# Two blocks' mixer projections as half products in the last input pass

## The chip, the cores and the metric

The kernel runs on one core of one Trainium2 chip. The metric is the device time of one execution in microseconds; lower is better. Times named "runs" are medians of several executions. The profile comes from one execution of its own.

## The reference

One layer of an encoder over 2048 tokens of width 1024. Attention and an mLSTM work side by side on a shared input projection; each has its own output projection and its own gate; their sum goes through w_out, and an FFN follows.

```python
xn = rms_norm(x, mix_norm_g)
proj = xn @ w_in
aq, ak, av, mq, mk, mv, mo, ipre, fpre, ga, gm = jnp.split(proj, points, axis=-1)
att = chunk_band_attention(aq, ak, av, rel_bias)            # (2048, 512)
mlstm_out = sigmoid(mo) * rms_norm(mlstm_chunkwise(...))    # (2048, 512)
y = sigmoid(ga) * (att @ w_att_proj) + sigmoid(gm) * (mlstm_out @ w_mlstm_proj)
x = x + y @ w_out
x = x + square(relu(rms_norm(x) @ w_up)) @ w_down
return rms_norm(x, final_norm_g)
```

All is float32. The change is about the two products `att @ w_att_proj` and `mlstm_out @ w_mlstm_proj`, each of 512 by 1024 weights, for the first 1024 tokens.

## The kernel before

**Tiling.** The tokens are four blocks of 512 (0 to 3); blocks 0 and 1 are stage s = 0, blocks 2 and 3 are s = 1. Activations lie feature by token in tiles of 128 x 512. A float32 factor is kept as two parts, a rounded one (ScalarE's cast) and the rest (a subtraction on VectorE), and each product is three matmuls: high by high, high by low, low by high. An `r` tile holds both parts of one operand row, a `wsp` tile both parts of 1024 weight columns. Splitting costs a ScalarE and a VectorE operation, for weights (L501, L503) as for activations (L1109 with L1114, or with a factor of a half L1111 with L1116).

**Seven products.** Most big products are made for two blocks at once by seven products of half-size operands instead of eight: the weights and the activations are each cut into 2 x 2, sums and differences of the parts are formed, seven products are accumulated in three kinds of banks (x, y and z of PLACES), and the four results a11, a12, a22 and a21 come out of `combine` with three ScalarE copies and three VectorE adds for each row tile. Sums of weights are made on the chip ahead of time by `sum_w` (from the table SUMS: pass and item at which the work is started, priority 3) and put into DRAM (`wsum`). Sums of activations are made by `take_parts`: for one k it takes five tiles, makes four loads one after the other, forms four sums, and hands seven parts to a splitter.

**The order of work.** A planner (class Flow) runs at build time. Every piece of work is a generator that asks for an engine with an assumed duration, for buffers from a pool, or for an event; the planner gives engines to the request that can start first, with a priority, and the instructions are written in that order; some reordering afterwards is left to the layer beneath. A load asks for the SP queue for 0.8 us (256 KB) and counts as landed 2 us later, so loads that follow one another in one generator are planned 2.8 us apart. TensorE's main work is one generator, `dense`, with the lowest priority; attention and the mLSTM recurrence (`mixers`) fill in between.

**The stages.** `dense` begins with v for blocks 0 and 1, then nine quads of the first input stage (IN_FIRST), then `in_far`, the second input stage: ten items (IN_ORDER: gm0, gm1, q, mq, vm, ga0, k, mk, ga1, mo) in three passes (g = 0, 1, 2), with products 0, 3 and 1, then 2 and 4, then 5 and 6. Half results between the passes are parked in DRAM and brought back by `unpark`, one after the other, with at most `room` tiles ahead. The activations of a pass sit in `ring`, 16 of the 28 r tiles. During the passes, the mixers of blocks 0 and 1 run, and their results are stored row by row in DRAM (`keep_mix`, L1298).

**The projections.** PROJ_IN puts the projection of block 0 before item 6 of pass 1 and that of block 1 before item 5 of pass 2. `project` (L562 to L564 through `pair_tile`) takes eight split rows (`take_mix`, `load_mix`, `take_u1`), goes over eight weight tiles of 24 matmuls, and `merge` (L992, L1000) multiplies with the gates, adds the branches and stores y. After block 1's, `take_y` (L1715, L1765, L1111, L1116) is started for four k to make the operands of w_out's quads (L631), which follow `in_far`. For k = 2 and 3 it brings the parts 0 and 1 first (`ahead`).

**Pools.** There are 28 r tiles (`rpool`), 16 `ctx` tiles, six `temp`, four `sc`, three `wsp`, four `wraw` (weights as loaded), and eight PSUM banks.

## Time and profile before

| what | value |
|---|---|
| time, median of 3 runs | 2738.43 us (2737.99 to 2741.09) |
| time of the profiled execution | 2734.73 us |
| its span in the profile | 2732.9 us |
| PE busy | 2717.4 us, 12832 matmuls |
| DVE (VectorE) busy | 2074.9 us |
| ACT (ScalarE) busy | 1527.6 us |
| DMA | 672.53 MB, mean 246 GB/s |

How to read it: PE is TensorE's matmul, PEld its weight load, SP the engine that issues nearly all DMAs. Busy time is the time in which an engine has an instruction in work. A row of a group reads: line, engine, operation, output <- inputs, tile sizes, count | busy us, mean ns of one | idle us before them and what ended most of it. A row of the waits reads: who waited at which line <- for whom: us in all, times, longest. A row of the timeline gives start, duration, engine, line, operation and tiles. A row of the stretches gives, after the bounds and length in us, the busy us and instruction counts of PE, PEld, DVE, ACT and POOL, TensorE's granted clock (1.00 is full), the share of time the DMA engines are busy, and GB/s.

### The profile page before, as it was taken

The numbers are of one execution on the slowest core, as the hardware profiler recorded it, in microseconds if no ns is written. First come the engines' busy times: TensorE is split into PE (matmuls) and PEld (weight loads), VectorE is DVE, ScalarE is ACT, GpSimd is POOL, SyncE is SP. The second block draws the span as 40 slices with busy tenths as digits, with TensorE's granted clock in tenths as the row PEclk, the third lists the DMA queues.
The fourth block names the chain that finished last, engine by engine and source line by source line (L and its number), as shares of the span: only waits on it lengthen the run. The fifth ranks groups of instructions, "written<-read, shape, count | busy, mean of one in ns | idle before, by whom it ended". The sixth has DMA issues, their size and how long they took to land.

```text
span 2732.9 us, 38055 instructions
## 1 busy us (share of the span) xinstructions
PE 2717.4 (99%) x12832; PEld 2262.6 (83%) x12832; DVE 2074.9 (76%) x3685; ACT 1527.6 (56%) x2650; POOL 48.2 (2%) x79
## 2 busy tenths in 40 slices
PE   9999999999999999999999999999999999999998
PEld 8878888888888888888888888888888888888887
DVE  7868776788875778897767798879888665657675
ACT  6545446676742534566556776666445565554443
POOL 0000000000000000000000000000000000000000
PEclk9999999999999999999999999999999999999999
DMA  8877678888868889767768876877774454588863
GB/s 297 280 257 259 243 266 280 269 250 266 281 215 271 306 307 303 239 216 261 254 230 279 277 254 204 255 229 245 252 233 160 154 204 158 185 276 272 286 234 138
DMA packets 331240, 672.53 MB, mean 246 GB/s; under 512 B 36788, under 2 KB 66100, under 8 KB 331044
## 3 DMA queue, kind: packets, MB, share of 16 engines
q1 hardware_dynamic: 330324, 669.03, 73.0%
q8 instruction: 101, 1.65, 0.2%
q10 hardware_dynamic: 720, 1.06, 0.1%
q14 instruction: 95, 0.78, 0.1%
HBM read 458.27 MB, written 211.68 MB: 245 GB/s over the span
## 4 chain that ended last, share of the span: by engine, by line
PE 90%; DVE 6%; issue 1%; DMA 1%; ACT 1%; POOL 0%; SPq 0%; POOLq 0%; DVEq 0%; ACTq 0%
PE bank L631 37%; PE bank L662 11%; PE bank L562 9%; PE bank L563 9%; PE bank L564 9%; PE bank L667 3%; PE bank L1337 2%; PE bank L1262 2%; PE bank L1369 2%; PE bank L856 1%; DVE wsp L503 1%; DVE r L1114 1%; DMA x<-ctx 1%; PE bank L1420 1%; PE bank L1597 1%
## 5 line engine op out<-in xcount | busy, mean ns | idle before, releaser
L631 PE MATMUL bank<-r,wsp 128*128 128x512 f32 x4872 | 1110.6, 390 | 1.9 <-ACT r L1109 1.1
L631 PEld LDWEIGHTS bank<-r,wsp 128*128 128x128 f32 x4872 | 912.6, 188 | 194.9 <-ACT r L1109 1.8
L501 ACT CAST wsp<-wraw 128x1024 fp32r<-128x1024 f32 x439 | 461.3, 1051 | 540.9 <-PE bank L563 203.7
L503 DVE TENSOR_TENSOR wsp<-wraw,wsp 128x1024 fp32r<-128x1024 f32 x439 | 536.1, 1221 | 277.8 <-ACT wsp L501 271.8
L562 PE MATMUL bank<-r,wsp 128*128 128x512 f32 x1088 | 430.4, 396 | 0.0
L563 PE MATMUL bank<-r,wsp 128*128 128x512 f32 x1088 | 425.0, 391 | 1.6 <-DVE r L1287 1.6
L564 PE MATMUL bank<-r,wsp 128*128 128x512 f32 x1088 | 424.7, 390 | 0.0
L662 PE MATMUL bank<-r,wsp 128*128 128x512 f32 x1512 | 368.5, 393 | 1.3 <-DVE ctx L755 0.8
L662 PEld LDWEIGHTS bank<-r,wsp 128*128 128x128 f32 x1512 | 278.9, 188 | 58.3 <-DVE ctx L755 1.5
L564 PEld LDWEIGHTS bank<-r,wsp 128*128 128x128 f32 x1088 | 204.2, 188 | 43.6
L563 PEld LDWEIGHTS bank<-r,wsp 128*128 128x128 f32 x1088 | 204.6, 188 | 40.4 <-DVE r L1287 2.0
L562 PEld LDWEIGHTS bank<-r,wsp 128*128 128x128 f32 x1088 | 204.3, 188 | 38.5 <-DVE r L1374 0.3
L1114 DVE TENSOR_TENSOR r<-r 128x512 fp32r<-128x512 f32 x271 | 179.8, 688 | 16.1 <-ACT r L1109 13.4
L1109 ACT CAST r<-r 128x512 fp32r<-128x512 f32 x271 | 157.9, 617 | 31.0 <-DMA r<-u 27.6
L1798 DVE TENSOR_TENSOR ctx<-bank,ctx 128x512 f32<-128x512 f32 x150 | 103.0, 687 | 64.1 <-PE bank L631 64.0
L520 DVE TENSOR_TENSOR wraw<-wraw,wraw 128x1024 f32<-128x1024 f32 x112 | 136.2, 1219 | 3.8 <-DMA wsum<-wraw 2.8
L1350 ACT ACTIVATE sc<-sc,scs 128x640 f32<-128x640 f32 (+4 forms) x128 | 97.5, 762 | 67.1 <-DVE scs L1343 66.4
L2119 ACT ACTIVATE ctx<-ctx 128x512 f32<-128x512 f32 x96 | 60.5, 630 | 105.7 <-DVE ctx L1798 105.6
L1790 ACT COPY ctx<-bank 128x512 f32<-128x512 f32 x150 | 87.3, 582 | 53.4 <-PE bank L631 51.3
L1374 DVE TENSOR_TENSOR r<-bank,r 128x512 fp32r<-128x512 f32 (+1 forms) x168 | 95.6, 593 | 14.5 <-ACT r L1372 13.8
L1372 ACT CAST r<-bank 128x512 fp32r<-128x512 f32 (+1 forms) x168 | 80.9, 515 | 31.3 <-PE bank L1369 29.3
L1262 PE MATMUL bank<-r,r 128*128 128x512 f32 x336 | 95.2, 365 | 0.0
(257 smaller groups left out, 3060.6 us busy)
## 6 DMA issues: line engine op xcount, KB each, us to landing
wraw<-in_wf SPq DMA_DIRECT2D x196, 512.0 KB, 4.4
r<-u SPq DMA_DIRECT2D x224, 256.0 KB, 4.2
wraw<-wsum SPq DMA_DIRECT2D x104, 512.0 KB, 4.5
u<-ctx SPq DMA_DIRECT2D x128, 256.0 KB, 2.4
u<-tmp SPq DMA_DIRECT2D x96, 256.0 KB, 2.4
wraw<-in_w SPq DMA_DIRECT2D x47, 512.0 KB, 4.4
ctx<-in_wf SPq DMA_DIRECT2D x88, 256.0 KB, 3.9
wsum<-ctx SPq DMA_DIRECT2D x88, 256.0 KB, 3.4
```

The source lines that it names most:

```text
L501: nc.scalar.copy(w[:, 0], raw)
L503: nc.vector.tensor_sub(w[:, 1], raw, w[:, 0].bitcast(F32))
L520: V.tensor_sub(dst, x, y)
L562: mm(ps, lh, rh, start=first, stop=False)
L563: mm(ps, lh, rl, start=False, stop=False)
L564: mm(ps, ll, rh, start=False, stop=last)
L631: mm(ps, wv[:, x, k, n], a[:, y], start=new and k == 0 and x == y == 0, stop=k == 3 and x == 1, skip_group_check=True)
L662: mm(ps, wv[:, x, k, n], a[:, y], start=start and x == y == 0, stop=stop and x == 1, skip_group_check=True)
L1109: self.nc.scalar.copy(dst[:, 0], src)
L1114: self.nc.vector.tensor_sub(dst[:, 1], src, dst[:, 0].bitcast(F32))
L1262: nc.tensor.matmul(bkv[:, :, c0:c0 + w], st, sl[:, :, o:o + w], start=n == 0, stop=n == total - 1)
L1798: nc.vector.tensor_add(t[:, o:o + 512], ps, t[:, o:o + 512])
```

## The change

The projections of blocks 0 and 1 are no longer made block by block. For each branch (x = 0 attention, x = 1 mLSTM) both blocks' rows are taken together as 2 x 2 parts, and seven products give the four results; as the contraction is only 512 long, a product has two k tiles instead of four, and two products share one weight tile. A branch is done in two halves q of the output columns. Branch 0 comes before item 1 (gm1) and branch 1 before item 4 (vm) of pass 2 (JOINT). The operands of both branches are made by `take_joint`, one branch and one k after the other, from the rows in DRAM, beginning with pass 2. The gated results of branch 0 are kept in four sc tiles and in six r tiles (through SP) until branch 1's are added. The sums of the two new weight matrices are made in the first input stage (SUMS at items 4 and 6). `take_y` becomes `take_y_late` for these blocks: each k waits until all seven parts of the k before it are there. The loads for pass 2's own products are started at the beginning of pass 1, and `unpark` may be eight tiles ahead in both passes, twelve after the second joint product.

```diff
@@ -46,7 +46,7 @@
 N_G, N_O, N_F = 2, 2, 8
 N_Q = N_G + N_O + 2 * N_F
 
-Q_VM = N_Q
+Q_VM, Q_PJ = N_Q, N_Q + 9
 Q_IN = dict(q=N_Q + 2, mq=N_Q + 3, ga0=N_Q + 4, k=N_Q + 5, mk=N_Q + 6, ga1=N_Q + 7, mo=N_Q + 8, gm0=0, gm1=1)
 IN_FIRST = ("gm0", "q", "mq", "ga0", "k", "mk", "gm1", "mo", "ga1")
 IN_ORDER = ("gm0", "gm1", "q", "mq", "vm", "ga0", "k", "mk", "ga1", "mo")
@@ -57,7 +57,8 @@
 
 SUMS = {(0, n): q for n, q in enumerate((Q_IN[IN_FIRST[0]], Q_VM, Q_VM + 1))}
 SUMS.update({at: N_Q - N_F + n for n, at in enumerate(((1, 1), (1, 6), *((4, i) for i in range(6))))})
-PROJ_IN = {(1, 6): 0, (2, 5): 1}
+SUMS.update({(0, 4): N_Q + 9, (0, 6): N_Q + 10})
+JOINT = {(2, 1): 0, (2, 4): 1}
 PROJ = {2: (4, 0), 3: (6, 0)}
 
 ORDER = (0, 1, 3, 2, 5, 4, 6)
@@ -359,8 +360,8 @@
             yield "quad", (Q_IN[name], True)
         for g, batch in enumerate(BATCHES):
             for i, name in enumerate(IN_ORDER):
-                if (g, i) in PROJ_IN:
-                    yield from project()
+                if (g, i) in JOINT:
+                    yield from (("half", (JOINT[g, i], t)) for t in range(7))
                 for m in (0, 1, 3) if name == "vm" and g == 0 else batch:
                     if name == "vm":
                         yield from (part(Q_VM + kk, m) for kk in range(2))
@@ -389,6 +390,19 @@
                     raws.append(raw)
                     fl.spawn(self.load_w(io["wf"][n[0], j], raw, evs[j]), 0)
                 i += 7
+                continue
+            if kind == "half":
+                x, t = n
+                q = Q_PJ + x
+                yield "wait", self.td_ev[q]
+                (raw,) = yield "get", self.wraw, 1
+                srcs = []
+                for h in (2 * t, 2 * t + 1):
+                    given, m = PARTS[h % 7]
+                    c = h // 7 * 512
+                    srcs.append((io["wf"][q], self.td[q].ap())[given][m][:, c:c + 512])
+                fl.spawn(self.split_turned(i, srcs, raw), 0)
+                i += 1
                 continue
             if kind == "turned":
                 c, kk, m = n
@@ -682,20 +696,21 @@
             if g > 0:
                 got, gev, room = ahead
             if g == 1:
-                fl.spawn(self.take_mix(0, ring), 1)
+                fl.spawn(self.take_batch(BATCHES[2], A, aev, ring), 1)
+            if g == 2:
+                fl.put(self.rpool, *(yield "get", ring, 8))
+                J = [self.operands() for _ in range(2)]
+                slots = (yield "get", self.sc, 4), (yield "get", self.rpool, 6), [[Event(), Event()] for _ in range(6)]
+                fl.spawn(self.take_joint(0, J), 1)
             for i, name in enumerate(IN_ORDER):
                 self.sum_at(g + 1, i)
                 if g < 2 and i == len(IN_ORDER) - 1:
-                    ahead = pair(lambda: [None] * NT), pair(E4), Pool([0] * (4 + 4 * g))
+                    ahead = pair(lambda: [None] * NT), pair(E4), Pool([0] * 8)
                     fl.spawn(self.unpark(g + 1, kept, *ahead), 1)
-                if (g, i) in PROJ_IN:
-                    b = PROJ_IN[g, i]
-                    yield from self.project(b, ring)
-                    if b == 0:
-                        fl.spawn(self.take_batch(BATCHES[2], A, aev, ring), 1)
-                        fl.spawn(self.take_mix(1, ring), 1)
-                    else:
-                        fl.put(self.rpool, *(yield "get", ring, 8))
+                if (g, i) in JOINT:
+                    yield from self.joint(0, JOINT[g, i], J, slots)
+                    if JOINT[g, i] == 1:
+                        fl.put(room, *[0] * 4)
                 tok = name == "vm"
                 finish, o = (self.after_vm(), 0) if tok else (self.after_in(1, name), off(name))
                 release = ring if i == len(IN_ORDER) - 1 else None
@@ -968,6 +983,131 @@
             O = self.y_operands = self.operands()
             for k in range(4):
                 fl.spawn(self.take_y(b // 2, k, *O), 2)
+    def take_joint(self, s, J):
+
+        def row(x):
+            def load(b, j, a):
+                i = 4 * x + (j if j < 4 else j - 2)
+                yield "wait", [self.blk[2 * s + b]["mix_ev"][i]]
+                yield "sp", 800, 2000
+                self.nc.sync.dma_start(a, self.mixd.ap()[2 * s + b, i])
+
+            return load
+
+        for x in range(2):
+            for k in range(2):
+                yield from self.take_parts(row(x), 1.0, k, self.splitter(k, *J[x], 1.0), J[x][1], pool=self.ctx)
+
+    def joint(self, s, x, J, slots):
+
+        fl, mm = self.fl, self.nc.tensor.matmul
+        want, self.banks.want = self.banks.want, 0
+        at = [(q, w, n) for q in range(2) for w in ("a11", "a12", "a22", "a21") for n in range(2)]
+        got = {a: ([], Event()) for a in at}
+        kept = [(y[0][:, :512], None) for y in slots[0]]
+        kept += [(r.bitcast(F32)[:, y], ev) for r, evs in zip(slots[1], slots[2]) for y, ev in enumerate(evs)]
+        kept = dict(zip(at, kept))
+        room = Pool([0] * 4)
+        fl.spawn(self.joint_gates(s, x, at, got, room), 1)
+        if x:
+            fl.spawn(self.joint_done(s, slots), 1)
+        A, aev = J[x]
+        for q in range(2):
+            bank, clear = {}, {}
+            after = self.combine(self.after_joint(s, x, q, got, kept, room))
+            for m, z in enumerate(PLACES):
+                t = 7 * q + m
+                if t % 2 == 0:
+                    w = yield from self.next_w()
+                wv = w.rearrange("p a (t k n c) -> p a t k n c", t=2, k=2, n=2)
+                for n in range(2):
+                    new = (z, n) not in bank
+                    if new:
+                        (bank[z, n],) = yield "get", self.banks, 1
+                    else:
+                        yield "wait", [clear[z, n]]
+                    ps = bank[z, n]
+                    for k in range(2):
+                        yield "wait", [aev[m][k]]
+                        yield "pe", 681
+                        a = A[m][k]
+                        for u, v in ((0, 0), (0, 1), (1, 0)):
+                            mm(ps, wv[:, u, t % 2, k, n], a[:, v], start=new and k == u == v == 0,
+                               stop=k == u == 1, skip_group_check=True)
+                    clear[z, n] = after(m, n, ps)
+                if t % 2 == 1:
+                    fl.put(self.wsplit, w)
+                if q == 1:
+                    fl.put(self.rpool, *A[m][:2])
+        self.banks.want = want
+        if x == 1:
+            O = self.y_operands = self.operands()
+            for k in range(4):
+                fl.spawn(self.take_y_late(s, k, O), 2)
+
+    def take_y_late(self, s, k, O):
+        if k > 1:
+            yield "wait", [self.yp_ev[2 * s][k], self.yp_ev[2 * s][k + 4]]
+        if k > 0:
+            yield "wait", [O[1][m][k - 1] for m in range(7)]
+        yield from self.take_y(s, k, *O)
+
+    def joint_gates(self, s, x, at, got, room):
+        fl, nc = self.fl, self.nc
+        for q, w, n in at:
+            hi, h = WHERE[w]
+            b, j = 2 * s + h, 4 * hi + 2 * q + n
+            yield "get", room, 1
+            tiles, ev = got[q, w, n]
+            tiles += yield "get", self.temp, 1
+            fl.spawn(self.joint_load(self.gd[b].ap()[x, j], tiles[0][:, :512], self.g_ev[x, b, j], ev), 1)
+
+    def joint_load(self, src, dst, kept, ev):
+        yield "wait", [kept]
+        yield "sp", 800, 2000
+        self.nc.sync.dma_start(dst, src)
+        self.fl.set(ev)
+
+    def joint_done(self, s, slots):
+        fl = self.fl
+        j = lambda q: [self.yp_ev[2 * s + h][4 * hi + 2 * q + n] for h in range(2) for hi in range(2) for n in range(2)]
+        yield "wait", j(0)
+        fl.put(self.sc, *slots[0])
+        fl.put(self.rpool, *slots[1][:2])
+        yield "wait", j(1)
+        fl.put(self.rpool, *slots[1][2:])
+
+    def after_joint(self, s, x, q, got, kept, room):
+        fl, V = self.fl, self.nc.vector
+
+        def finish(n, which, t, ps):
+            tiles, ev = got[q, which, n]
+            hi, h = WHERE[which]
+            b, j = 2 * s + h, 4 * hi + 2 * q + n
+            old, moved = kept[q, which, n]
+            yield "wait", [ev]
+            g = tiles[0][:, :512]
+            yield "dve", dve_ns(574)
+            V.scalar_tensor_tensor(old if x == 0 and moved is None else g, g, 1.0, t[:, :512] if ps is None else ps,
+                                   op0=ALU.add, op1=ALU.mult)
+            fl.put(self.ctx, t)
+            if ps is not None:
+                fl.put(self.banks, ps)
+            fl.put(room, 0)
+            if x == 0 and moved is None:
+                fl.put(self.temp, tiles[0])
+                return
+            if x == 0:
+                fl.spawn(self.store(old, g, moved, self.temp, tiles[0], "sp!"), 1)
+                return
+            if moved is not None:
+                yield "wait", [moved]
+            yield "dve", dve_ns(512)
+            V.tensor_add(g, g, old)
+            fl.spawn(self.store(self.ypd[b].ap()[j], g, self.yp_ev[b][j], self.temp, tiles[0], "sp!"), 1)
+
+        return finish
+
     def load_gates(self, b, gates, go):
         fl = self.fl
         for j in range(KT):
@@ -1306,7 +1446,7 @@
             fl.set(B["mix_ev"][x])
             if self.direct(b, x):
                 fl.set(B["mixed"][x])
-            else:
+            elif b > 1:
                 fl.spawn(self.load_mix(b, x), 1)
 
     def direct(self, b, x):
...
+    for w in (w_att, w_ml):
+        w = w.reshape(4, P, KT, P)
+        quads.append(np.stack([np.concatenate([w[k:k + 2, :, c + o:c + o + 2].transpose(1, 0, 2, 3).reshape(P, 512)
+                                               for o in (0, 2)], axis=1) for k in (0, 2) for c in (0, 4)]))
```

More of the change, by code (lines that the diff above doesn't have):

```diff
@@ L2418, in build @@
         self.vdram = [nc.dram_tensor(f"vspill{b}", (NT, P, D), F32R, kind="Internal") for b in range(NB)]
-        self.td = [f32d(f"wsum{q}", 4, P, 1024) for q in range(N_Q + 9)]
+        self.td = [f32d(f"wsum{q}", 4, P, 1024) for q in range(N_Q + 11)]
         self.x2d = [f32d(f"x2_{b}", KT, P, T) for b in range(NB)]
```

## The prediction

> **What bounds the kernel now.** I read the page first, then the list of what PE waited for, then a table of stretches around the change, then single instructions.
>
> ```profile
> span 2732.9 us, 38055 instructions
> ...
> PE 2717.4 (99%) x12832; PEld 2262.6 (83%) x12832; DVE 2074.9 (76%) x3685; ACT 1527.6 (56%) x2650; POOL 48.2 (2%) x79
> ...
> DVE  7868776788875778897767798879888665657675
> ...
> PE 90%; DVE 6%; issue 1%; DMA 1%; ACT 1%; POOL 0%; SPq 0%; POOLq 0%; DVEq 0%; ACTq 0%
> ```
>
> TensorE (PE) is busy for 99% of the span and makes 90% of the chain that ended last; all its idle time together is 15.5 us. So matmuls taken out are time gained, one for one, as long as PE finds its operands, and every new wait of PE is lost one for one.
>
> ```profile
> PE bank L563 <- DVE r L1287: 1.6, 1, 1.6
> ```
>
> This is the longest wait in the list for PE: 1.6 us. The kernel before has no place where PE waits for operands of any size, so there is nothing to win back but the matmuls themselves.
>
> ```profile
> core 0: us, PE busy (x) PEld busy (x) DVE busy (x) ACT busy (x) POOL busy (x), PEclk, DMA share, GB/s
> 931.40:942.30 10.90, 10.90 (x50) 9.03 (x49) 8.31 (x12) 9.42 (x16) 0.00 (x0) 1.00 0.93 314
> 942.30:977.40 35.10, 35.10 (x158) 28.18 (x157) 24.47 (x38) 14.90 (x20) 0.00 (x0) 1.00 0.94 320
> 977.40:999.10 21.70, 21.70 (x97) 18.00 (x96) 17.22 (x27) 8.22 (x13) 0.00 (x0) 1.00 0.90 312
> 999.10:1042.70 43.60, 43.60 (x194) 36.08 (x194) 25.07 (x34) 10.56 (x14) 0.00 (x0) 1.00 0.88 308
> 1042.70:1097.30 54.60, 54.60 (x241) 44.93 (x240) 52.52 (x80) 34.25 (x51) 0.00 (x0) 1.00 0.88 294
> ```
>
> These five stretches are the last pass (g = 2) of the second input stage: gm0; gm1, q and mq; vm; the projection of block 1; and ga0 to mo. Two things stand beside the full PE here: the DMA engines are at 88 to 94% and move 294 to 320 GB/s, and VectorE (DVE) is at 96% in the last stretch. The change moves work into this pass.
>
> **Matmuls: what is removed.**
>
> ```profile
> 999.14 0.39 PE L562 MATMUL bank<-r,wsp 128*128 128x512 f32 x1
> ...
> 1042.66 0.61 PE L662 MATMUL bank<-r,wsp 128*128 128x512 f32 x2
> ```
>
> One projection starts at 999.14 and the next item at 1042.66: 8 tiles x 2 x 4 x 3 = 192 matmuls in 43.52 us, or 0.2267 us each. Before, two blocks take 384. After, each branch takes 2 halves x 7 products x 2 x 2 x 3 = 168, both 336. The 48 that go are worth 48 x 0.2267 = **-10.9 us**. The new ones have the same form. This is also the most that can be gained.
>
> **What the pass has to carry.** Without projection 1 the five stretches hold 165.9 - 43.6 = 122.3 us of PE; the joint products add 336 x 0.2267 = 76.2, together 198.5 us.
>
> Bytes: the five stretches moved 3.4 + 11.2 + 6.8 + 13.4 + 16.1 = 50.9 MB. Projection 1 has 8 weight tiles, 16 gates and 8 stores of y in it, 10.5 MB. The joint form brings 14 weight tiles (7.3), 32 gates (8.4), 16 operand rows (4.2), 12 half results parked (3.1) and 16 stores of y (4.2), 27.3 MB at 0.26 MB a tile and 0.52 a weight tile. That makes 67.7 MB in 198.5 us, 341 GB/s. The best stretch above has 320 at 94%. At 320 the pass takes 211.5 us, **13 us more than its matmuls**. Some loads can slip over the pass's ends, so I take this as a support for the waits below, not as a term.
>
> ```profile
> L503 DVE TENSOR_TENSOR wsp<-wraw,wsp 128x1024 fp32r<-128x1024 f32 x439 | 536.1, 1221 | 277.8 <-ACT wsp L501 271.8
> ...
> L1114 DVE TENSOR_TENSOR r<-r 128x512 fp32r<-128x512 f32 x271 | 179.8, 688 | 16.1 <-ACT r L1109 13.4
> L1109 ACT CAST r<-r 128x512 fp32r<-128x512 f32 x271 | 157.9, 617 | 31.0 <-DMA r<-u 27.6
> ```
>
> ```profile
> 1080.84 0.68 DVE L1765 TENSOR_TENSOR ctx<-ctx,ctx 128x512 f32<-128x512 f32 x1
> 1081.44 0.68 DVE L780 TENSOR_TENSOR ctx<-bank,ctx 128x512 f32<-128x512 f32 x1
> 1082.04 1.22 DVE L503 TENSOR_TENSOR wsp<-wraw,wsp 128x1024 fp32r<-128x1024 f32 x1
> 1083.17 0.75 DVE L1965 SCALAR_TENSOR_TENSOR ctx<-ctx,cvw,ctx 128x512 f32<-128x512 f32 x1
> 1083.84 0.68 DVE L780 TENSOR_TENSOR ctx<-bank,ctx 128x512 f32<-128x512 f32 x1
> 1084.44 0.68 DVE L1116 SCALAR_TENSOR_TENSOR r<-ctx,r 128x512 fp32r<-128x512 f32 x1
> ```
>
> VectorE: back to back, a 512-wide operation takes 0.60 us from start to start and a weight split 1.13. The joint form has 14 splits, 32 gate multiplies, 24 + 16 adds and 4 x 11 operand sums and splits: 116 x 0.60 + 14 x 1.13 = 85 us. With the 102.5 us that the other four stretches show, VectorE has 188 us to do in 198.5. Two weight tiles and 32 mix splits go, but those of block 0 and most of block 1 lay before this pass.
>
> **Wait 1, in front of the first joint product.** The loads of its operands are started at the pass's beginning, T, when eight r tiles come back; gm0 keeps PE for 10.9 us, then PE needs both k of the first product. Operands are prepared for k = 0 wholly, then k = 1: within each, four loads follow one another.
>
> ```profile
> L1715 SPq DMA_DIRECT2D ctx<-yp x4: 320/434/553, 1067.6 to 1076.3; - x4
> ```
>
> The same code made these four loads for the y operands: 8.7 us from the first to the fourth, and the add at 1080.84 above came 4.5 us after the fourth: 13.2. Then eleven VectorE operations at 0.60, 6.6: k = 0 is done at T + 19.8. If the loads of k = 1 have run ahead by then, its first part needs a cast and a subtraction, 0.62 + 0.69: T + 21.1. PE gets there at T + 10.9 and has 0.7 us of k = 0 to do: a wait of **9.5 us**. If k = 1's loads start only when k = 0 has given back its five ctx tiles, 13.2 more: 23. If casts and loads are hoisted ahead of their place,
>
> ```profile
> 549.62 0.27 PE L1369 MATMUL bank<-const,sc 128*128 128x128 f32 x1
> 549.64 0.71 PE L662 MATMUL bank<-r,wsp 128*128 128x512 f32 x2
> ```
>
> as on PE here, where two matmuls of a group of three follow a lone transpose, the wait may fall to some 3. I take **10**, near the middle bound: while PE stands, little else is queued on SP, ScalarE and VectorE. The mixers aren't late:
>
> ```profile
> 858.11 0.32 SPq L1298 DMA_DIRECT2D mix<-ctx  x1
> ```
>
> the last row of block 1 is stored at 858, and the pass begins at 931.4 - 43.6 = 888. For the second branch there are 32.7 us (gm1, q, mq) after the first, against the 21 of the chain: no wait.
>
> **Wait 2, in front of w_out.** The y operands are now made strictly one k after the other, behind the second joint product, with vm to mo (21.7 + 54.6 us) to hide them. There are 28 r tiles, eight of them hold the pass's operands until its last matmul. So k = 0 and 1 take 14, k = 2 gets six and its seventh only at the end, and k = 3 starts behind that: a cast and a subtraction (1.3), a load, another 1.3.
>
> ```profile
> tmp<-yp SPq DMA_DIRECT2D x8, 256.0 KB, 4.0
> ```
>
> That is 6.6 us and some issue time, less the 2.0 us in which PE works on k = 0 to 2 (9 matmuls): about **5**. It can be 0, if the seventh tile comes from the half of those eight that was read 5.4 us earlier and all moves up. It grows if k = 2 isn't done by then: a pass takes 13.2 + 6.6 = 19.8 us with VectorE free, 26.4 with half of it free; three are 79.2 against 76.3. With a third free they are 99, some 23 late. I take **7**.
>
> **The rest.** Two more weights get their sums in the first pass of stage one: 16 subtractions, 11 us of VectorE at 0.69, prio 3, 8 MB of DMA; the slices there show 7 to 8 tenths for VectorE, and that hides it (0; uncovered, up to 3). Gates, copies and stores of the joint products are off the path unless VectorE is late. I take **1** for all, between 0 and 5.
>
> Sum: -10.9 + 10 + 7 + 1 = **+7.1 us**. The profiled execution (2734.7 us, span 2732.9) would become 2741.8; the median of the runs lies 3.7 above it (2738.43), so the prediction is 2738.4 + 7.1 = 2745.5.
>
> [...] In the five stretches PEclk is 1.00, and no wait is longer than 1.6 us. [...]
>
> **The rivals.**
>
> *Operands come in time (faster, 0.20).* Waits of 3, 0 and 1 give -6.9: 2731.5. It decides if all waits together stay under 5.4 us. For it: the shown hoisting, and 858 against 888. Against it: 67.7 MB in 198.5 + 5.4 us is 332 GB/s, above any stretch here.
>
> *A draw (0.27).* The waits add up to between 5.4 and 16.4, for instance 9.5 + 1 + 0: 2738. It needs 315 to 332 GB/s, which the pass nearly shows.
>
> *The written order holds (slower, 0.13).* SP, ScalarE and VectorE keep the sequence of the code, and k = 1's loads wait for k = 0's tiles: 23, then 14 at w_out, 2 elsewhere: +28, 2766. For it: the four loads of 1067.6 to 1076.3 keep 2.9 us apart. Against it: a queue with nothing before it needn't keep such distances.
>
> [...]
>
> *The forecast itself: 0.32.* I see no way in which the matmul count isn't reduced.
>
> **How the numbers follow.** About 0.2%, 5.5 us, is what a measurement can tell from no change. Faster 0.20; within 0.27; slower 0.32 + 0.13 + 0.08 = 0.53. The range reaches from 2732, nearly the first rival (its better part, some 0.13, is left out), to 2764, just under the written order (0.07 left out). The forecast's own range, with waits of 16.4 to 24 us, is 2744 to 2752.
>
> **What would show it.** Right: PE's matmuls fall by 48, to about 12784; in the list of waits two new entries of PE appear, the joint line and the quads at w_out, both on the split of r tiles, about 10 and 7 us; the pass's DMA share is at 90% or more. Wrong: PE's idle total stays near 15 us (faster), or the waits are for weight splits, gates or parked tiles instead, or sit in the first pass.

## The result, and the profile after

| | before | after |
|---|---|---|
| median, us (21 runs each, lowest to highest) | 2736.68 (2734.57 to 2741.09) | 2742.26 (2738.85 to 2747.01) |
| ratio, 95% interval | | 1.0018 (1.0012 to 1.0024) |
| span of the profiled execution, us | 2732.9 | 2738.3 |
| matmuls | 12832 | 12784 |

The change costs 5.6 us by the medians, 4.9 by the ratio, 5.4 by the profiled spans, where +7.1 had been forecast. The three estimated terms of the sum are wrong, though, and cancel by chance. The page of the kernel after, its busy times, the slices of VectorE and the chain:

```profile
span 2738.3 us, 38122 instructions
...
PE 2712.4 (99%) x12784; PEld 2253.9 (82%) x12784; DVE 2109.3 (77%) x3747; ACT 1547.5 (57%) x2688; POOL 45.6 (2%) x79
...
DVE  7878776788876898896767788879888665657675
...
PE 81%; DVE 8%; DMA 4%; issue 4%; ACT 2%; SPq 1%; POOL 0%; POOLq 0%; DVEq 0%; ACTq 0%
```

48 matmuls are gone, and PE is busy for 5.0 us less, not 10.9. Its idle time went from 15.5 to 25.9 us, and the chain from 90% PE to 81%. So part of the loss is idle PE, and part is matmuls that took longer. What PE waited for, in the kernel after:

```profile
PE bank L1035 <- ACT r L1249: 2.5, 2, 2.0
PE bank L676 <- DVE ctx L795: 2.3, 3, 1.6
PE bank L577 <- DVE r L1427: 1.6, 1, 1.6
PE bank L676 <- DVE r L1514: 1.6, 1, 1.6
```

L1035 is the joint product's matmul, L1249 the cast of an operand. This is wait 1, at 2.5 us; no wait of the output quads (L645) stands at the top of the list, and from 1103 to 1140 us, where they begin, PE has no listed wait at all. Where the rest went is seen by stages. I cut both traces at the first ordinary product matmul of each pass of the second input stage, and behind the last one of the last pass (before, the second and the last pass hold a projection of 43.5 us each; after, the last holds all joint products):

| us | before | after | difference |
|---|---|---|---|
| first pass | 293.5 | 300.8 | +7.3 |
| second and last pass | 183.1 + 165.7 = 348.8 | 140.0 + 208.5 = 348.5 | -0.3 |
| from there to the end | 1635.8 | 1634.5 | -1.3 |

The 10.9 us of matmuls left the second and last pass, and these got only 0.3 us shorter: 10.6 us are missing there. Of these, 1.4 us are no loss: six matmuls of the output quads lie inside the last pass after (1097.3 to 1098.8 us), none before, which is also the -1.3 of the last row. The other 9 us were lost in the two passes. And 7.3 us were lost in the first pass, which the change seems not to touch. The last pass after, by windows: gm0; first half of the first joint branch; its second half with gm1, q and mq; the second branch; the rest in two:

```profile
core 0: us, PE busy (x) PEld busy (x) DVE busy (x) ACT busy (x) POOL busy (x), PEclk, DMA share, GB/s
895.40:906.30 10.90, 10.90 (x50) 9.03 (x49) 9.00 (x13) 7.88 (x12) 0.00 (x0) 1.00 0.88 293
906.30:930.00 23.70, 21.16 (x84) 16.26 (x83) 18.39 (x28) 12.29 (x20) 0.00 (x0) 0.93 0.68 218
930.00:979.60 49.60, 49.51 (x218) 39.48 (x218) 44.12 (x67) 25.09 (x37) 0.00 (x0) 1.00 0.89 310
979.60:1024.10 44.50, 44.34 (x196) 36.36 (x196) 43.68 (x68) 19.94 (x28) 0.00 (x0) 1.00 0.93 312
1024.10:1060.00 35.90, 34.34 (x152) 28.15 (x151) 29.40 (x46) 15.48 (x26) 0.00 (x0) 1.00 0.92 317
1060.00:1103.90 43.90, 43.27 (x191) 35.29 (x190) 41.79 (x63) 26.51 (x41) 0.00 (x0) 1.00 0.96 342
```

The second row is the only one far from its matmuls: 84 x 0.2267 = 19.0 us, and it lasts 23.7, with a granted clock of 0.93 in place of 1.00. The two last rows lose some 2 us together. The instructions there:

```profile
880.02 0.32 SPq L993 DMA_DIRECT2D ctx<-mix  x1
...
893.17 0.45 SPq L993 DMA_DIRECT2D ctx<-mix  x1
903.82 0.32 SPq L993 DMA_DIRECT2D ctx<-mix  x1
...
906.28 0.84 PE L1035 MATMUL bank<-r,wsp 128*128 128x512 f32 x3
909.08 10.30 PE L1035 MATMUL bank<-r,wsp 128*128 128x512 f32 x37 [1.96 <-ACT r L1249]
```

The four loads for k = 0 are issued from 880.0 to 893.2, before the pass begins at 895.4 and so ahead of their place in the code (what let them run ahead, the planner or the layer beneath it, was not tested); those for k = 1 start at 903.8. So PE does three matmuls of k = 0 and stands for 1.96 us. Then 37 matmuls take 10.30 us, 1.9 more than 37 x 0.2267. The first seven start 0.23 to 0.34 us apart; from 910.6 on eight starts are 0.43 us apart, and then the pace is 0.23 again. There is another short wait, 0.58 us, before 919.97. The stretch of the wait and the one behind it in the windows view:

```profile
907.15:910.56 3.41, 1.48 (x6) 1.24 (x7) 1.17 (x3) 2.15 (x4) 0.00 (x0) 1.00 0.88 326
910.56:913.98 3.42, 3.42 (x9) 2.64 (x8) 3.42 (x6) 1.50 (x3) 0.00 (x0) 0.50 0.60 183
```

The granted clock in the second is 0.50. Idle and half pace cost about the same.

Two theories stood at this point. **Operands**: the joint products' operands come late, as forecast, and the first pass's loss is a side effect. **Sums**: the two new weight sums (priority 3, taken as hidden) are the larger cost, and they fall in the first stage and the first pass.

### The profile page after: what moved, and what is told of

Its sections match the earlier page's. It is cut to its first block, busy times and chain, and to the rows that moved or that the text cites. A ratio compares the mean times of both kernels' runs of the same rounds, so it can differ in the third digit from the quotient of the medians.

```text
span 2738.3 us, 38122 instructions
## 1 busy us (share of the span) xinstructions
PE 2712.4 (99%) x12784; PEld 2253.9 (82%) x12784; DVE 2109.3 (77%) x3747; ACT 1547.5 (57%) x2688; POOL 45.6 (2%) x79
## 4 chain that ended last, share of the span: by engine, by line
PE 81%; DVE 8%; DMA 4%; issue 4%; ACT 2%; SPq 1%; POOL 0%; POOLq 0%; DVEq 0%; ACTq 0%
PE bank L645 36%; PE bank L676 9%; PE bank L576 8%; PE bank L577 8%; PE bank L578 8%; PE bank L681 2%; PE bank L1035 2%; PE bank L1477 2%; PE bank L1509 2%; PE bank L1402 2%; DVE wsp L517 2%; PE bank L871 1%; DVE r L1254 1%; DVE ctx L1905 1%; DMA ctx<-mix 1%
## 5 line engine op out<-in xcount | busy, mean ns | idle before, releaser
L645 PE MATMUL bank<-r,wsp 128*128 128x512 f32 x4872 | 1110.2, 389 | 1.9 <-ACT r L1249 1.4
L645 PEld LDWEIGHTS bank<-r,wsp 128*128 128x128 f32 x4872 | 913.0, 188 | 193.8 <-ACT r L1249 2.1
L576 PE MATMUL bank<-r,wsp 128*128 128x512 f32 x960 | 380.5, 397 | 0.0
L577 PE MATMUL bank<-r,wsp 128*128 128x512 f32 x960 | 375.1, 391 | 1.6 <-DVE r L1427 1.6
L578 PE MATMUL bank<-r,wsp 128*128 128x512 f32 x960 | 375.0, 391 | 0.0
L676 PE MATMUL bank<-r,wsp 128*128 128x512 f32 x1512 | 369.1, 394 | 4.1 <-DVE ctx L795 2.3
L676 PEld LDWEIGHTS bank<-r,wsp 128*128 128x128 f32 x1512 | 278.8, 188 | 62.2 <-issue 3.3
L578 PEld LDWEIGHTS bank<-r,wsp 128*128 128x128 f32 x960 | 180.2, 188 | 38.8
L577 PEld LDWEIGHTS bank<-r,wsp 128*128 128x128 f32 x960 | 180.6, 188 | 35.4 <-DVE r L1427 2.1
L576 PEld LDWEIGHTS bank<-r,wsp 128*128 128x128 f32 x960 | 180.3, 188 | 33.5 <-DVE r L1514 0.4
L1254 DVE TENSOR_TENSOR r<-r 128x512 fp32r<-128x512 f32 x255 | 169.2, 689 | 16.7 <-ACT r L1249 14.3
L1938 DVE TENSOR_TENSOR ctx<-bank,ctx 128x512 f32<-128x512 f32 x174 | 119.3, 687 | 64.6 <-PE bank L645 61.5
L1249 ACT CAST r<-r 128x512 fp32r<-128x512 f32 x255 | 148.8, 617 | 28.0 <-DMA r<-u 27.1
L1930 ACT COPY ctx<-bank 128x512 f32<-128x512 f32 x174 | 101.1, 583 | 74.1 <-PE bank L645 53.7
```

The source lines that it names most:

```text
L576: mm(ps, lh, rh, start=first, stop=False)
L577: mm(ps, lh, rl, start=False, stop=False)
L578: mm(ps, ll, rh, start=False, stop=last)
L645: mm(ps, wv[:, x, k, n], a[:, y], start=new and k == 0 and x == y == 0, stop=k == 3 and x == 1, skip_group_check=True)
L676: mm(ps, wv[:, x, k, n], a[:, y], start=start and x == y == 0, stop=stop and x == 1, skip_group_check=True)
L1249: self.nc.scalar.copy(dst[:, 0], src)
```

## The experiments

In what follows a difference is the difference of the ratios to the kernel before, times 2737 us; each carries some 3 us of uncertainty.

**1. The change without its two sums.**

```diff
-SUMS.update({(0, 4): N_Q + 9, (0, 6): N_Q + 10})
-                yield "wait", self.td_ev[q]
-                    srcs.append((io["wf"][q], self.td[q].ap())[given][m][:, c:c + 512])
+                    srcs.append(io["wf"][q][m][:, c:c + 512])
```

> The changed kernel without the two sums of the projection weights: the joint products read raw weights in their place (that part of the computation is left out). If the sums, which run late and fall into pass 0 among the mixers, cost the 7.6 us by which passes 0 and 1 grew (433.1 to 440.7 us), then passes 0 and 1 take 433 to 435 us and the time is 5.5 - 7.5 = about 2 us under before. If the growth comes from the projection that was taken out of pass 1, or from the different order of everything, they stay near 440 us and the time about 5 us above before.

Measured: 2731.38 us, ratio 0.9975 (0.9965 to 0.9984), 11.8 us below the changed kernel. The first pass is 293.2 again, the first half of the joint branch 22.5.

**2. The kernel before with the two sums, which nothing reads.**

```diff
+SUMS.update({(0, 4): N_Q + 9, (0, 6): N_Q + 10})
...
-        self.td = [f32d(f"wsum{q}", 4, P, 1024) for q in range(N_Q + 9)]
+        self.td = [f32d(f"wsum{q}", 4, P, 1024) for q in range(N_Q + 11)]
```

> The kernel before, with only the two sums added at the same places; nobody reads them. If the sums are the cause, the time is 5 to 8 us above before and the growth lies in pass 0 (before: 748.3 - 454.8 = 293.5 us). If not, it stays within 1.5 us of before.

Measured: 2745.25 us, ratio 1.0026 (1.0016 to 1.0036): the sums alone cost 7.1 us in a kernel that has no joint product. The first pass is 298.8, the last 168.6 (before: 293.5 and 165.7).

**3. The first joint branch one product group later.**

```diff
-JOINT = {(2, 1): 0, (2, 4): 1}
+JOINT = {(2, 2): 0, (2, 4): 1}
```

> The changed kernel with the first joint product one item later (before q in place of gm1, 10.9 us more for its operands). If the wait in front of it is that of the operand chain, its loss of about 5 us (2.1 us idle, eight matmuls at half pace, 1 us more) goes and the time is 0 to 2 us above before. If the pass is bound by transfers, the loss reappears later in the pass (908.7 - 895.4 against 198 us of matmuls) and the time stays about 5 us above.

Measured: 2746.2 us, ratio 1.0034 (1.0022 to 1.0047), slower than the change as it is. Wait 1 does shrink with the time that the operands get: the first half of the branch takes 20.9 us in place of 24.0, from its first matmul to the first of the second half. The last pass became 2.6 us shorter, 205.9, but the stretch behind it 8.6 us longer. The longest entry in the list of what PE waited for:

```profile
PE bank L645 <- ACT r L1251: 4.4, 2, 3.4
```

PE's instructions at that place, in order of time:

```profile
1110.03 1.88 PE L645 MATMUL bank<-r,wsp 128*128 128x512 f32 x7 [0.22 <-DVE r L1256]
1115.27 3.22 PE L645 MATMUL bank<-r,wsp 128*128 128x512 f32 x6 [3.37 <-ACT r L1251]
```

Wait 2 exists: with the first joint branch closer to the end, the output quads stand for 4.4 us, and then six matmuls take 3.22 us (the view ends there; the granted clock is 0.93 from 1101.3 to 1147.5 us) where seven took 1.88 just before. In the change as it is, the same place, in the same view, runs through:

```profile
1104.08 18.08 PE L645 MATMUL bank<-r,wsp 128*128 128x512 f32 x79
```

79 matmuls without a break, although the loads of k = 3 are issued only from 1107.4 to 1111.3. PE works on the parts of other products that need k = 0 to 2 meanwhile.

**4. The two sums in the second pass, at its first and third group.**

```diff
-SUMS.update({(0, 4): N_Q + 9, (0, 6): N_Q + 10})
+SUMS.update({(2, 0): N_Q + 9, (2, 2): N_Q + 10})
```

> The changed kernel with the two sums started in pass 1 (items 0 and 2), where attention is done. If the sums in pass 0 are the cause, pass 0 takes 293 to 295 us again and the time is 0 to 2 us under before, unless the sums come too late for the joint products' weights (a wait of PE for a weight split in front of the first joint product). If they are not the cause, the time stays about 5 us above before.

Measured: 2750.25 us, ratio 1.0042 (1.0030 to 1.0055). The first pass is back at 293.8, but the second takes 156.4 in place of 140.0, with a wait of 4.9 us for a load into a ctx tile and a granted clock of 0.90 from 800 to 850 us, which is 5 us of lost pace. The cost follows the sums, and here it is larger.

**5. The two sums earlier, at priority 1, so that they end before the first pass.**

```diff
-SUMS.update({(0, 4): N_Q + 9, (0, 6): N_Q + 10})
+SUMS.update({(0, 3): N_Q + 9, (0, 4): N_Q + 10})
-            self.fl.spawn(self.sum_w(SUMS[stage, i]), 3)
+            self.fl.spawn(self.sum_w(SUMS[stage, i]), 1 if stage == 0 and i > 2 else 3)
```

> The changed kernel with its two sums started one and two items earlier in the first stage (items 3 and 4) and with priority 1 in place of 3. If it is their place in pass 0 that costs 7 us, and they now end before pass 0 begins (455), pass 0 takes 293 to 295 us and the time is about 6 us under before, as without them (2731). If the work as such costs (VectorE and DMA time wherever it lies), the loss moves into the first stage: 455 becomes 460 or more, and the time stays 3 to 6 us above before.

Measured: 2748.8 us, ratio 1.0035 (1.0023 to 1.0048). The last subtraction of the two sums ran at 366 us, and still the first pass took 309.2 and the second 135.0. Some of that is work moved between the two (the first holds 17 more matmuls than in the change as it is); together they take 444.2, 3.5 more than in the change. So my reading "it costs because it lies in the first pass" failed in this form. What the sums displaced is seen in the split of the first pass's operands (L1254), in the windows 380 to 455 and 455 to 620 (VectorE's busy time on this line and its instructions, clock, DMA). The kernel after:

```profile
380.00:455.00 75.00, 10.51 (x16) 1.00 0.91 311
455.00:620.00 165.00, 0.00 (x0) 1.00 0.87 271
```

This one:

```profile
380.00:455.00 75.00, 1.89 (x3) 1.00 0.86 288
455.00:620.00 165.00, 8.51 (x13) 0.99 0.82 257
```

Thirteen of sixteen splits slid into the first pass. Work at priority 1 had pushed out what the pass needs.

**6. Operands of the first branch made for k = 0 and k = 1 at once**, k = 1 through other scratch tiles.

```diff
-        for x in range(2):
-            for k in range(2):
-                yield from self.take_parts(row(x), 1.0, k, self.splitter(k, *J[x], 1.0), J[x][1], pool=self.ctx)
+        self.fl.spawn(self.take_parts(row(0), 1.0, 1, self.splitter(1, *J[0], 1.0), J[0][1], pool=self.temp), 1)
+        yield from self.take_parts(row(0), 1.0, 0, self.splitter(0, *J[0], 1.0), J[0][1], pool=self.ctx)
+        yield "wait", [J[0][1][m][1] for m in range(7)]
+        for k in range(2):
+            yield from self.take_parts(row(1), 1.0, k, self.splitter(k, *J[1], 1.0), J[1][1], pool=self.ctx)
```

> The changed kernel in which both k of the first branch's operands are made side by side, the second in temp tiles in place of ctx tiles. If the wait in front of the first joint product is the chain of one k after the other, the first half of that product (84 matmuls, 23.9 us from 906.3 to 930.0 in place of 19.0) takes 19 to 20 us and the time falls by 4 to 5 us, to about before. If transfers bound it (317 GB/s in the stretch before), the time changes by less than 2 us.

Measured: 2738.13 us, ratio 1.0003 (0.9994 to 1.0012), 4.1 us below the change. The last pass takes 201.2 us, the first half of the joint branch 20.0 in place of 23.7. The same pass, by the same six items:

```profile
893.60:904.50 10.90, 10.90 (x49) 9.02 (x49) 8.55 (x12) 8.31 (x14) 0.00 (x0) 1.00 0.84 278
904.50:924.50 20.00, 19.69 (x85) 15.48 (x84) 19.75 (x31) 10.92 (x19) 0.00 (x0) 1.00 0.86 285
924.50:973.90 49.40, 49.26 (x218) 39.32 (x217) 43.35 (x65) 25.04 (x39) 0.00 (x0) 1.00 0.92 314
973.90:1018.40 44.50, 44.28 (x195) 36.24 (x194) 44.04 (x69) 20.11 (x28) 0.00 (x0) 1.00 0.90 304
1018.40:1060.00 41.60, 41.60 (x185) 34.44 (x185) 35.97 (x55) 19.21 (x31) 0.00 (x0) 1.00 0.96 340
1060.00:1094.80 34.80, 34.80 (x155) 28.78 (x154) 33.72 (x53) 21.78 (x33) 0.00 (x0) 1.00 0.95 332
```

The clock is 1.00 throughout, and PE is full in the last two rows at 340 and 332 GB/s. The pass is within 3 us of the 198.5 us of its matmuls. The profiled execution was the fastest of the eleven, 2732.38 us, so its trace shows this kernel at its best.

**7. Experiments 5 and 6 together** (both diffs above).

> Both edits of the two runs before this one. If the two losses are separate, they add: 7 + 4.5 us better than the changed kernel, that is about 6 to 7 us under before plus 4: 2727. If the pass is bound by transfers, the second edit adds nothing to the first.

Measured: 2745.07 us, ratio 1.0023 (1.0014 to 1.0032), 3.3 us below experiment 5; first pass 308.6, last 201.3. Both k at once are worth the same here, and the early sums stay bad.

**8. Experiments 1 and 6 together** (both diffs above).

> The changed kernel with the operands of the first joint branch made for k=0 and k=1 at once, and without the two new weight sums (it reads the raw weights in their place, so the sums of the joint weights are left out of what it computes). If the two costs are separate, they add: the sums are 10.9 us below the changed kernel and the operands 4.1, so it is 15 us below the changed kernel and 9 to 11 us faster than before, about 2727; the stretch of the first input pass is 293, of the last 200 to 201. If the wait for operands shrinks by itself when the sums are gone, so that one and the same disturbance was counted twice, it is about where the kernel without the sums was: 5 to 7 us faster than before, 2731.

Measured: 2729.69 us, ratio 0.9972 (0.9963 to 0.9981), 12.6 us below the change, where 15 (by these ratios 15.9) would be additive and 11.8 is experiment 1 alone. The first half of the joint branch went from 22.5 to 20.2. The last pass takes 204.8 us, not the 200 to 201 of separate costs. The runs do not tell the two outcomes apart; what both k at once take off wait 1 is at any rate smaller without the sums, 2.3 us by the trace.

**9. The kernel before with the first of the two sums alone** (experiment 2 with `SUMS.update({(0, 4): N_Q + 9})`).

> The kernel before with one of the two new weight sums alone, the one of the first stage's fifth slot, which nothing reads. If it is the second sum that costs (its four scratch tiles are taken at about 400 us and come back at about 528, beside the mixers of the first input pass), this one costs nothing: within 1 us of before, the first pass 293 to 295 long. If any work for VectorE and the queues in the first stage delays the operands of the first pass, half or more of the 7 us is here: 3 to 5 us slower than before, the first pass 297 or more.

Measured: 2737.66 us, ratio 1.0002 (0.9993 to 1.0011), first pass 293.8. The first sum costs nothing; the second, of the seventh slot, costs the 7 us. The stretch 455 to 600 us in the windows view, in this kernel:

```profile
455.00:600.00 145.00, 143.75 (x787) 121.72 (x786) 113.49 (x319) 104.20 (x252) 7.29 (x13) 1.00 0.85 261
```

The same stretch in the kernel of experiment 2:

```profile
455.00:600.00 145.00, 143.07 (x771) 119.34 (x770) 115.21 (x312) 101.04 (x244) 7.26 (x13) 1.00 0.86 268
```

With the second sum VectorE is busy for only 1.7 us more in this stretch and the DMA engines for hardly more (0.86 against 0.85), and yet PE gets 16 matmuls less done and VectorE seven instructions less. The sum issued its first load at 381 us and its last store at 528, and the one that used to lie there began at 529. So the first pass holds three sums in place of two. No single wait is longer than 1.0 us there; PE loses some tenths of a us at many places. Over the whole first pass, measured by the usual distance from one matmul of a form to the next, PE's matmuls come late by more than 0.08 us at 103 places in experiment 2 and at 77 here, and by 16.8 and 12.2 us in all. The four waits listed in that pass of experiment 2 are for operands of the mixers (scores, transposes, recurrence).

**10. Both k at once, the new sums in the first pass's two slots, the two displaced sums of the last weights at the end of the wide stage.**

```diff
-SUMS.update({at: N_Q - N_F + n for n, at in enumerate(((1, 1), (1, 6), *((4, i) for i in range(6))))})
-SUMS.update({(0, 4): N_Q + 9, (0, 6): N_Q + 10})
+SUMS.update({(4, i): N_Q - N_F + i for i in range(8)})
+SUMS.update({(1, 1): N_Q + 9, (1, 6): N_Q + 10})
```

> The changed kernel with both k at once, with the two new sums in the two slots of the first input pass in which two sums of the last weights were made, and these two in the seventh and eighth slot of the wide stage behind, where the six others are. If the new sums cost because they come on top of a full first stage and first pass, nothing is on top there any more: the first pass is 292 to 295, and the wide stage takes the two at 0 to 2 us, so it is 5 to 7 us below the kernel with both k at once: about 2731 to 2733, faster than before by 4 to 6 us. If a sum costs its 3 to 4 us wherever it lies, the cost moves to the wide stage: 2737 to 2739, the stretch behind the last pass 6 us or more longer.

Measured: 2743.74 us, ratio 1.0027 (1.0017 to 1.0037). Half of it came as expected: the first pass is 293.3, the three passes together 635.0 (before 642.3, after 649.3). But the stretch behind them grew by 16.4 us against experiment 6: these two sums now lie at 1535 to 1677 us, beside the mixers of the second half. The granted clock is 0.58 from 1680 to 1692 us, 5 us of lost pace. PE there:

```profile
1681.50 0.68 PE L1793 MATMUL bank<-const,ctx 128*128 128x128 f32 x4 [2.88 <-DVE ctx L1783]
...
1686.80 0.80 PE L576 MATMUL bank<-r,wsp 128*128 128x512 f32 x1 [2.91 <-ACT wsp L515]
...
1689.53 0.63 PE L577 MATMUL bank<-r,wsp 128*128 128x512 f32 x1
1689.95 0.63 PE L578 MATMUL bank<-r,wsp 128*128 128x512 f32 x1
```

**11. The kernel before with the same move of its two sums** (`SUMS.update({(4, i): N_Q - N_F + i for i in range(8)})`).

> The kernel before with its two sums of the first input pass moved to the seventh and eighth slot of the wide stage, which leaves the first pass without any. If the two sums of that pass are hidden in the kernel before, this moves nothing: within 1.5 us of before. If each sum in that pass costs 3 us or so, as the two new ones did, the first pass gets 4 to 7 us shorter (287 to 290) and the kernel faster by as much, less what the wide stage takes.

Measured: 2754.18 us, ratio 1.0060 (1.0048 to 1.0073). The first two passes take 477.0 us together without any sum in the first, 476.6 with two: two sums there are hidden. (The first alone takes 299.0 in place of 293.5, because 24 more matmuls lie in it that the second then has fewer of.) The end grew by 16.1 us here too. Experiments 10 and 11 have the sums of the last weights at the same places, and differ by the joint form (with both k at once) and its two sums: 9.0 us, close to the 10.9 of the matmuls.

**12. Both k at once, and no stage with a third sum**: one new sum in the first stage (free by experiment 9), the other in the first pass's first slot; one of the last weights' sums goes in front of the output quads.

```diff
+enumerate(((1, 6), (5, 0), (4, 0), (4, 1), (4, 2), (4, 3), (4, 4), (4, 5)))})
+SUMS.update({(0, 4): N_Q + 9, (1, 1): N_Q + 10})
...
+                if s == 0:
+                    self.sum_at(5, i)
```

> The changed kernel with both k at once and with no pass and no wide stage holding more sums than in the kernel before: one new sum in the first stage's fifth slot, where the kernel before with it alone was 0.2 us off; the other new one in the first of the two slots of the first input pass; the last weights' sum of the second of these slots stays, the one that gives up its slot goes between the last input pass and the wide stage, in front of the output products. If the second new sum costs because it makes a third one in the first pass, the first two passes together are 432 us (441 in the changed kernel) and the time is 6 to 8 us below the kernel with both k at once: 2730 to 2732, faster than before by 5 to 7 us. If the first stage's sum and the first pass's hurt each other even so, the first two passes stay at 438 or more and the time at 2736 to 2738. If the sum in front of the output products delays their operands, the passes are short and the stretch behind the last pass grows by 2 to 6 us: 2732 to 2736.

Measured: 2735.64 us, ratio 0.9990 (0.9980 to 0.9999): 2.7 us faster than before, with the interval just short of 1, and 7.7 us below the change. The first two passes take 432.1 us (293.3 + 138.8), as the first outcome has it: with two sums in the first pass, one of them new, its loss is gone. The price is paid as in the third outcome: the stretch behind the last pass grew by 7.2 us. The 48.2 us behind the last pass in the windows of experiment 6:

```profile
1094.80:1143.00 48.20, 47.83 (x209) 38.63 (x209) 42.61 (x55) 22.09 (x30) 0.00 (x0) 1.00 0.87 287
```

And in those of this one, with PE's instructions in the middle of it:

```profile
1091.80:1140.00 48.20, 44.87 (x185) 35.05 (x184) 40.86 (x57) 19.38 (x26) 0.00 (x0) 0.96 0.93 314
```

```profile
1113.81 0.73 PE L645 MATMUL bank<-r,wsp 128*128 128x512 f32 x2 [0.70 <-ACT r L1255]
1115.49 3.88 PE L645 MATMUL bank<-r,wsp 128*128 128x512 f32 x9 [0.94 <-DVE r L1260]
```

24 matmuls less in the same time, 24 x 0.2267 = 5.4 us: the quads wait for the split of their operands (L1255, L1260), beside which the sum now lies (its subtractions run from 1103 to 1129 us). That is wait 2 again; that the sum is what delays the splits is inferred from its place.

## Why the prediction was right in its total and wrong in its terms

**Matmuls, -10.9: right.** 48 are gone. Experiments 10 and 11, equal in the placement of the last weights' sums, differ by 9.0 us.

**Wait 1, +10: right place, half the size.** The wait is there, on the cast of the operand's k = 1, and the first half of the branch takes 4.7 us more than its matmuls; both k at once take away 2.3 to 4.5 us of this by the traces (1 and 8, after and 6, 5 and 7), and 10.9 us more time for the operands 3.1 (3). The step that failed is "the loads of its operands are started at the pass's beginning": those of k = 0 were issued up to 15 us earlier. I had quoted such hoisting for PE and allowed for it only as a lower bound of 3. Of the 4.7 us only 2.5 are listed as a wait; most of the rest is half pace, eight matmuls at 0.20 us more each.

**Wait 2, +7: not there as the change stands.** The failing step is the cover, "less the 2.0 us in which PE works on k = 0 to 2": 79 matmuls ran without a break, as parts of other products were drawn ahead. The mechanism isn't wrong, only not reached: a later first branch (3) or one more sum beside the quads (12) brings it out, at 8.6 us behind the last pass over the change and 7.2 over experiment 6.

**The rest, +1: the largest miss.** "The slices there show 7 to 8 tenths for VectorE, and that hides it" failed. The sums cost 7.1 us alone (2) and 11.8 in the change (1). My upper bound was 3. The sums also ran elsewhere than the sentence has them: the first one's subtractions lay at 308 to 391 us, in the first stage, the second one's at 467 to 526 us, in the first pass. I had counted the engine's free time, and it was free; what counts is that with a third sum in the pass the mixers' chains come late. I also asked only whether the sums' own time was covered, not what they push to a later place: the sum whose subtractions lay at 494 to 541 us moved to 538 to 585. The runs show that the first pass has its old length with two sums in it, old or new (9, 10, 12), and is 5 to 7 us longer with three (2, after). Two things stay open. Which resource carries the delay (scratch tiles held for long, VectorE's order or the queues) isn't settled. And the third sum was each time the one begun in the seventh slot of the first stage; no run has it there beside only one other, so the number of sums and the place of this one aren't told apart.

**Bytes: wrong.** "13 us more than its matmuls", from a best rate of 320 GB/s, isn't so: the rows of experiment 6 have 340 and 332 GB/s with PE full. The highest rate seen in a kernel that needs less is no ceiling. VectorE's 188 us were right: the six rows of the last pass after add up to 186.4.

**The rivals.** "Operands come in time" needed waits under 5.4 us, and the waits for operands were: alone this would have made the kernel faster, as experiment 1 is. The 0.08 among the chances of slower rests on nothing that the run before shows; the run after has eight matmuls 0.43 us apart in place of 0.23, behind the one wait of 1.96 us. The outcome lies just inside the 0.2% that I called the resolution, with 1.0012 as its lower end; so "no change to speak of" and "slower" are both fair to it, and the number 2745.5 was near it because a wait of 7 us that didn't come stood in for sums of 7 us or more that did. By the runs the sum is -10.9 + 4.7 + 0 + 11.8 = +5.6, where the last term carries its 3 us.

**What would show it.** The matmuls and the first wait came as described, the wait at a quarter of its size in the list (2.5 for 10); the DMA share of the pass was 0.89; the second wait didn't come; and "sit in the first pass" was on the list of what would prove it wrong, and did.

## What to carry to other kernels

Background work at low priority is not free because its engine has idle time: count how much of it is already in a stage, and look at what it pushes into the next one. Here two such sums in a pass were free, a third, begun in the stage before, cost 7 us, in another stage two cost 16, and one in the first stage nothing. And estimate a wait from where the queue really issues the loads, and from all the matmuls that can be put ahead of a late operand, not from the order of the code.

## What the runs showed of the hardware

PE ran some matmuls behind a wait at half pace. After, eight starts from 910.6 us on lie 0.43 us apart in place of 0.23, behind an idle time of 1.96 us; the granted clock is 0.50 from 910.56 to 913.98 us and 0.93 in the second window of the last pass. In experiment 3 six matmuls took 3.22 us behind 3.37 us, and the clock is 0.93 from 1101.3 to 1147.5 us. In experiment 10 the starts lie 0.43 us apart behind waits of 2.88 and 2.91 us, and the clock is 0.58 from 1680 to 1692 us. In experiment 12 nine matmuls took 3.88 us behind waits of 0.70 and 0.94 us that lay 1.7 us apart, and the clock is 0.96 in the 48.2 us behind its last pass.

Behind other waits it did not: in experiment 6 three matmuls took 0.96 us right behind one of 2.27 us, and the next nine of the same line 2.23 us. After, PE stood for 1.63, 1.56 and 1.63 us in the windows 755 to 770, 1045 to 1060 and 1945 to 1960 us, and the clock is 1.00 in each. So in these traces the length of the one wait doesn't decide; what does was not shown.

The eight matmuls at half pace after cost 8 x 0.20 = 1.6 us, nearly as much as the 1.96 us before them, and the list of waits (2.5 us in two for L1035) doesn't hold it.
